# Which pairs of a SwiGLU projection use seven products, and where their fourth sum and their gated product stand

## The chip, the core and the metric

The kernel runs on one core of a Trainium2 chip. The metric is the time of one execution in microseconds (us), as the device measures it. A profile of one execution comes with its own time and its span, which is the time from the first instruction to the last. Times without a unit below are microseconds. TensorE (PE) multiplies matrices, and its weight loads are listed as PEld. VectorE is DVE, ScalarE is ACT, GpSimd is POOL, and SyncE (SP) issues most of the loads. Each of them works through its own queue of instructions.

## The reference

One layer of a streaming encoder for 256 positions of a new stream and 64 positions of a running one, 320 columns in all, with 2048 features. The part that the change touches is the feed-forward block:

```python
h = x + merged @ w_out[l]
hn = rmsnorm(h, norm_ffn[l])
gu = hn @ w_gate_up[l]
h = h + (jax.nn.silu(gu[..., :D_FF]) * gu[..., D_FF:]) @ w_down[l]
```

`D_FF` is 5632, so `w_gate_up` has 44 blocks of 128 gate columns and 44 of 128 up columns, and `w_down` has 44 blocks of 128 rows. All values are float32.

## The kernel before

Features lie on the 128 partitions and the 320 positions in the free dimension. float32 precision is made from 16-bit numbers: each weight block is scaled by a power of two and split into a high half (ScalarE, `Group.high`, line 373) and a low half (VectorE, `Group.low`, line 376), and the activations likewise. A product of a 128 x 128 block is then three matmuls of 320 columns, high by high, high by low, low by high (`product`, lines 108 to 110).

The feed-forward part works through 44 **pairs**, each a block of gate columns and the block of up columns that goes with it, over 16 blocks of input features. They are cut into three slices of 16, 16 and 12 pairs. Behind the first three pairs of the next slice (`AHEAD`) comes the down projection of a slice: 16 blocks, each with 16 (or 12) blocks of weights. Below, pair 1.4 is pair 4 of slice 1, counted from 0 within its slice; that is also how the table `FAST` counts.

An **ordinary** pair is a `Group` of two units: 2 x 16 x 3 = 96 matmuls of 320 columns. A pair in `FAST` is a `Fast`, a **seven-product** pair: two-by-two blocks of weights and activations are multiplied with seven products in place of eight, in the terms that hold the two low halves. It has 32 matmuls of 320 columns (`whole`, line 416) and seven times 16 of 160 columns (`cross`, line 422). Four of the seven products have sums of weight blocks as weights, made on VectorE by `sum_up` (line 412). Sums 1, 2 and 3 are made when the pair begins. Sum 4 is written over sum 2, so it cannot begin before the matmuls of product 2 have read that; product 22 at the end of the pair reads sum 4. When the pair is done, `join` (lines 454 to 459) adds the pieces up, ScalarE makes the silu, and `out` (line 1178, or 1180 for an ordinary pair) multiplies gate by up and takes the maximum of it (line 206).

The order is written by the program itself. A step (`tick`) is 8 blocks of input features in a product, four to a pair. `at(step, fn, rank)` puts a function down for a later step, and within a step the functions run in the order of their ranks; what they issue goes to the end of each engine's queue. So for a pair that begins at step S: the loads 10 or 11 steps ahead, a bound of each unit two steps later (ScalarE, line 210, into the unused `junk`), the maximum and its rounding (`topmost`, `packed`, lines 216 and 218) at S - 7 for a seven-product pair and S - 6 for an ordinary one, a small matmul that spreads it over the partitions into the one buffer `row` (line 222) at S - 5 or S - 4, then `peak`, `down`, `up` (lines 226 to 228), the high halves (rank 2) and the low ones (rank 2). `gated` runs one step behind the end of a pair (rank 2), and `out` one step behind that (rank 3). When a slice's last product is made, its maxima are spread in the same way and its activations are split, three in a step, on ScalarE and VectorE (lines 170 and 171).

Of the kernel before, what the change touches and what calls it, by code (L numbers as in the profile page):

```python
# [16 lines left out]
P = 128  # L17
# [6 lines left out]
HALF = 8  # L24
# [6 lines left out]
QSCALE = 128.0 ** -0.5  # L31
WARM = 10
PLAIN = 3
FAST = (7, 9, 10, 12, 13, 15), (2, 4, 5, 7, 8, 10, 11, 13, 14), (2, 4, 5, 7, 8, 10, 11)
AHEAD = 3
BACK = 4
WHOLE = 6
# [14 lines left out]
def stream_step(ctx: ExitStack, tc: tile.TileContext, xT, w_in, w_a, w_b, w_out, w_gu, w_down,  # L52
# [10 lines left out]
    def acc():  # L63
        return psum.tile([P, 512], F32, tag="acc", bufs=3, name="acc")

    def aux():
        return psum.tile([P, 512], F32, tag="aux", bufs=4, name="aux")
# [8 lines left out]
    def at(tick, fn, *a, rank=5):  # L76
        if tick <= state["tick"]:
            fn(*a)
        else:
            later.setdefault(tick, []).append((rank, fn, a))  # L80

    def tick():
        state["tick"] += 1
        for _, fn, a in sorted(later.pop(state["tick"], ()), key=lambda x: x[0]):
            fn(*a)

    def after(n, fn, *a, rank=5):
        if n == 0:
            fn(*a)
        else:  # L90
            at(state["tick"] + n, fn, *a, rank=rank)
# [53 lines left out]
    def slot(shape=(T,), dt=F32R, name="S"):  # L145
        return big.tile([P, *shape], dt, tag="S", bufs=SLOTS, name=name)
# [28 lines left out]
    def t320(tag, bufs=2, dt=F32):  # L175
        return tmp.tile([P, T], dt, tag=tag, bufs=bufs, name=tag)
# [212 lines left out]
    class Fast(Group):  # L389
# [35 lines left out]
        def blocks(self, x):  # L425
            assert state["tick"] == self.start
            gate, up, more = acc(), aux(), aux()
            part = lambda ps, n: ps[:, n * N : (n + 1) * N]
            turn_of["seen"] = turn_of.get("seen", 0) + 1
            self.seen = tmp.tile([P, 2, N], F32, tag="seen" if turn_of["seen"] % 2 else "sq", bufs=1, name="seen")  # L430
            self.chain, self.other, self.third = (part(more, n) for n in range(3))
            w0, w1, s, mid = self.w[0][2], self.w[1][2], self.sums, HALF // 2
            at(self.start + 1, lambda: nc.scalar.copy(out=self.seen[:, 0], in_=self.chain), rank=0.8)
            self.cross(self.chain, w0, 0, x, 11, start=True, stop=True)
            self.whole(gate, 0, x)
            tick()
            self.whole(up, 1, x)
            self.cross(part(up, 0), w1, HALF, x, 4, stop=True)
            tick()
            self.cross(self.chain, s[2], 0, x, 2, stop=True)  # L440
            self.sum_up(4, w0[:, :, HALF * P :], s[2], s[2])
            self.cross(part(gate, 0), w0, HALF, x, 21)
            self.cross(self.other, s[1], 0, x, 1, range(0, mid), start=True)
            tick()
            self.cross(self.other, s[1], 0, x, 1, range(mid, HALF), stop=True)
            self.cross(self.third, s[3], 0, x, 3, start=True, stop=True)
            self.cross(part(gate, 1), s[4], 0, x, 22, stop=True)
            tick()
            return gate[:, :T], up[:, :T]
# [453 lines left out]
    for i, (kind, n) in enumerate(line):  # L903
        by_vector = (0,) if 4 <= i < 33 and i % 5 in (1, 3) or i > 40 and i % 3 == 2 else ()
        if kind == "in":
            g = Group([[(w_in[n][:, j * HALF * P : (j + 1) * HALF * P], HALF) for j in range(2)]], start, lambda: [mixed.undo], 11, by_vector)
        else:
            g = Group([[(w_a[n], H), (w_b[n], H)]], start, lambda: [aT.undo, bT.undo], 11, by_vector, True)
# [129 lines left out]
    for g in range(H):  # L1038
        ps, undo = block16(3 * H + g, mixed.half)
        at(state["tick"] + 1, lambda g=g, ps=ps, undo=undo: nc.scalar.activation(  # L1040
            out=us[g], in_=ps, func=AF.Gelu_apprx_tanh, scale=undo), rank=2)
# [24 lines left out]
    for m in range(KD):  # L1066
        g = groups.pop(("ab", m))
# [23 lines left out]
    for made, (kind, s, i) in enumerate(order):  # L1091
        s0, n = SLICES[s]
        pieces = lambda w, k0, n: [(w[:, (k0 + k) * P : (k0 + min(k + HALF, n)) * P], min(HALF, n - k)) for k in range(0, n, HALF)]
        if kind == "up":
            if i < PLAIN:
                groups[kind, s, i] = Plain(w_gu[i], KD, now), Plain(w_gu[KF + i], KD, now + 2)
            else:
                both = [pieces(w_gu[i], 0, KD), pieces(w_gu[KF + i], 0, KD)]
                if i - s0 in FAST[s]:
                    groups[kind, s, i] = Fast((w_gu[i], w_gu[KF + i]), now, lambda: [ffn.undo])  # L1100
                else:
                    groups[kind, s, i] = Group(both, now, lambda: [ffn.undo], 12 if i < FAST[0][0] else 11, (), tight=i >= FAST[0][0])
            now += 4
        else:
            if i % 2 == 0:
                g = Group([pieces(w_down[i], s0, n), pieces(w_down[i + 1], s0, n)], now, lambda s=s: [acts[s].undo], 11, (), True, True)
# [21 lines left out]
    for m in range(KD):  # L1128
        x = t320("ev")
# [31 lines left out]
    def gated(s, pg, pu, g):  # L1161
        t, u = t320("ev"), t320("bb")
        if g is None:
            nc.vector.tensor_tensor(out=t, in0=pg, in1=got["rh"], op=ALU.mult)
            nc.scalar.activation(out=t, in_=t, func=AF.Silu)
            nc.vector.tensor_tensor(out=u, in0=pu, in1=got["rh"], op=ALU.mult)
        else:
            fast = isinstance(g, Fast)
            if fast:
                g.join(pg, pu, t, u)  # L1170
            nc.scalar.activation(out=t, in_=t if fast else pg, func=AF.Silu, scale=g.undo)
            if not fast:
                nc.scalar.activation(out=u, in_=pu, func=AF.Copy, scale=g.undo)

        def out():
            r = slot(dt=F32, name="act")
            if isinstance(g, Fast):
                nc.vector.scalar_tensor_tensor(out=r, in0=u, scalar=g.undo, in1=t, op0=ALU.mult, op1=ALU.mult)
            else:
                nc.vector.tensor_tensor(out=r, in0=u, in1=t, op=ALU.mult)  # L1180
            acts[s].add(r)

        after(1, out, rank=3)

    def downed(s, i, ps, g):
        nc.vector.scalar_tensor_tensor(out=hs[i], in0=ps, scalar=g.undo, in1=hs[i], op0=ALU.mult, op1=ALU.add)
# [18 lines left out]
    for kind, s, i in order:  # L1205
        if kind == "up":
            if i < PLAIN:
                gate_w, up_w = groups.pop((kind, s, i))
                pg, pu, g = gate_w.block(hg), up_w.block(hg), None
            else:  # L1210
                g = groups.pop((kind, s, i))
                pg, pu = g.blocks(ffn) if isinstance(g, Fast) else (g.block(0, ffn.half), g.block(1, ffn.half))
            at(state["tick"] + 1, gated, s, pg, pu, g, rank=2)
            continue
        end = s == 2 and i == KD - 1
        g, u = groups.pop((kind, s, i))
# [147 lines left out]
```

## Time and profile before

| | us |
|---|---|
| median of 3 runs | 1599.82 (1599.57 to 1601.29) |
| the profiled execution, its own time | 1598.27 |
| its span | 1596.5 |
| TensorE busy (matmul) | 1573.1, 99% of the span |
| VectorE busy | 1198.5, 75% |
| ScalarE busy | 1090.8, 68% |
| granted TensorE clock, mean | 0.997 |

The busy time of matmuls is modelled: each is shown longer than the time until the next one begins, since they overlap. What a piece of work takes on TensorE is therefore read from the starts of matmuls, and an idle time in brackets is counted from the modelled end of the matmul before. In a row of the timeline stand the start, the time shown, the engine, the line, the operation, the tile written and those read, the shapes and how many, and in brackets the idle time ahead of it with what ended that.

### The profile page before, as it was taken

The page shows a single profiled execution, that of the slowest core. Times are in us where ns is not written, and L with a number is a line of the kernel's source. Part 1 is how long each engine was busy: PE and PEld are TensorE (multiplying, and loading weights), DVE is VectorE, ACT ScalarE, POOL GpSimd, SP SyncE. Part 2 cuts the span into 40 slices and gives each one's busy share as a digit, 9 for nine tenths or more (in the row PEclk, how much of TensorE's full clock was granted, in tenths as well). Part 3 has the DMA queues.
Part 4 walks back from the last instruction along what each step waited for, and adds up shares of the span by engine and source line. Part 5 has one row for each costly group of instructions (what it writes and reads, how often), then busy time and mean ns, then how long its engine had stood idle before and what let it go on. Part 6 is the DMA issues. An engine that isn't in the chain of part 4 may idle for free.

```text
span 1596.5 us, 30559 instructions
## 1 busy us (share of the span) xinstructions
PE 1573.1 (99%) x12759; PEld 1232.9 (77%) x12759; DVE 1198.5 (75%) x2097; ACT 1090.8 (68%) x1229; POOL 68.1 (4%) x80
## 2 busy tenths in 40 slices
PE   9999999999999999999999999999999999999997
PEld 9987777777777768879778877778888777788775
DVE  6789887977777766966968878557888765688775
ACT  6589888867556654846776677666776776666663
POOL 0110111100000000121000000000000000000000
PEclk9999999999999999999999999999999999999998
DMA  8567665654444444554544454444545544444441
GB/s 304 200 202 221 198 173 147 190 167 159 159 159 158 160 141 162 184 176 170 185 169 167 170 183 141 163 164 143 174 169 178 166 159 158 159 159 148 146 130 66
DMA packets 94186, 268.49 MB, mean 168 GB/s; under 512 B 28288, under 2 KB 34688, under 8 KB 88416
## 3 DMA queue, kind: packets, MB, share of 16 engines
q1 hardware_dynamic: 91600, 261.36, 49.6%
q0 software_dynamic: 1312, 3.80, 0.6%
q8 instruction: 99, 1.62, 0.4%
q10 hardware_dynamic: 1136, 1.39, 0.2%
q14 instruction: 39, 0.32, 0.1%
HBM read 256.03 MB, written 5.51 MB: 164 GB/s over the span
## 4 chain that ended last, share of the span: by engine, by line
PE 80%; DVE 11%; ACT 6%; issue 3%; DMA 1%; DVEq 0%; POOL 0%; SPq 0%; ACTq 0%
PE acc L108 23%; PE acc L110 23%; PE acc L109 23%; DVE w L376 4%; DVE sum L412 3%; PE aux L422 3%; ACT w L373 2%; PE aux L539 2%; PE aux L416 1%; PE acc L416 1%; PE acc L422 1%; ACT junk L210 1%; PE acc L539 1%; DVE tops L206 1%; DVE half L171 1%
## 5 line engine op out<-in xcount | busy, mean ns | idle before, releaser
L110 PE MATMUL acc<-half,w 128*128 128x320 f16 x2688 | 803.7, 299 | 1.2 <-DVE w L376 1.1
L108 PE MATMUL acc<-half,w 128*128 128x320 f16 x2688 | 803.8, 299 | 0.4 <-DVE gate L1054 0.3
L109 PE MATMUL acc<-half,w 128*128 128x320 f16 x2688 | 803.7, 299 | 0.0
L373 ACT ACTIVATE w<-raw,up 128x2048 f16<-128x2048 f32 (+1 forms) x216 | 425.4, 1970 | 313.7 <-PE acc L110 210.0
L376 DVE SCALAR_TENSOR_TENSOR w<-raw,up,w 128x2048 f16<-128x2048 f32 (+1 forms) x216 | 499.0, 2310 | 99.3 <-ACT w L373 97.3
L210 ACT ACTIVATE junk<-raw 128x2048 uint8<-128x2048 f32 (+1 forms) x190 | 354.3, 1865 | 5.7 <-DMA raw<-w_in 1.7
L110 PEld LDWEIGHTS <-w 128*128 128x128 f16 x2688 | 263.0, 98 | 103.8 <-DVE w L376 1.8
L108 PEld LDWEIGHTS <-w 128*128 128x128 f16 x2688 | 263.0, 98 | 103.7 <-issue 2.0
L109 PEld LDWEIGHTS <-w 128*128 128x128 f16 x2688 | 263.0, 98 | 97.5 <-issue 0.9
L226 DVE TENSOR_REDUCE peak<-row 128x1 f32<-128x128 f32 x159 | 45.7, 288 | 123.9 <-PE row L222 123.9
L422 PEld LDWEIGHTS <-sum 128*128 128x128 f16 x1408 | 98.5, 98 | 9.1 <-DVE sum L412 9.1
L416 PEld LDWEIGHTS <-w 128*128 128x128 f16 x704 | 68.3, 98 | 25.1
L422 PE MATMUL aux<-mix,sum 128*128 128x160 f16 x1056 | 80.7, 233 | 0.0
L422 PEld LDWEIGHTS <-w 128*128 128x128 f16 x1056 | 75.7, 98 | 2.5
L130 ACT CAST w<-raw 128x1024 fp32r<-128x1024 f32 x36 | 37.7, 1047 | 42.6 <-PE acc L110 29.5
L206 DVE TENSOR_REDUCE tops<-raw 128x1 f32<-128x2048 f32 x26 | 59.2, 2277 | 0.0
L412 DVE TENSOR_TENSOR sum<-w,sum 128x2048 f16<-128x2048 f16 x44 | 53.8, 1223 | 5.9 <-PE aux L422 4.5
L412 DVE TENSOR_TENSOR sum<-w 128x2048 f16<-128x2048 f16 x44 | 53.6, 1219 | 1.0
L416 PE MATMUL aux<-half,w 128*128 128x320 f16 x352 | 51.4, 299 | 0.0
L416 PE MATMUL acc<-half,w 128*128 128x320 f16 x352 | 51.4, 299 | 0.0
L133 DVE TENSOR_TENSOR w<-raw,w 128x1024 fp32r<-128x1024 f32 x36 | 44.4, 1236 | 5.0 <-ACT w L130 4.7
L108 PE MATMUL acc<-S,w 128*128 128x320 f32 x144 | 44.8, 311 | 0.0
(256 smaller groups left out, 1641.6 us busy)
## 6 DMA issues: line engine op xcount, KB each, us to landing
raw<-w_in SPq DMA_DIRECT2D x141, 512.0 KB, 4.7
raw<-w_gu SPq DMA_DIRECT2D x88, 512.0 KB, 4.6
raw<-w_gu SPq DMA_DIRECT2D x44, 1024.0 KB, 4.8
raw<-w_down SPq DMA_DIRECT2D x80, 512.0 KB, 4.0
raw<-w_out SPq DMA_DIRECT2D x32, 512.0 KB, 4.7
raw<-w_a SPq DMA_DIRECT2D x16, 512.0 KB, 3.6
raw<-w_b SPq DMA_DIRECT2D x16, 512.0 KB, 4.5
raw<-w_down SPq DMA_DIRECT2D x16, 256.0 KB, 4.0
```

The costliest lines, as they stand in the source:

```text
L108: nc.tensor.matmul(ps[:, :T], a, x[0], start=first, stop=False, skip_group_check=True)
L109: nc.tensor.matmul(ps[:, :T], a, x[1], start=False, stop=False, skip_group_check=True)
L110: nc.tensor.matmul(ps[:, :T], b, x[0], start=False, stop=last, skip_group_check=True)
L206: nc.vector.tensor_reduce(out=self.tops[:, i : i + 1], in_=src, axis=mybir.AxisListType.X, op=ALU.max, apply_absolute_value=True)
L210: nc.scalar.activation(out=junk, in_=src, func=AF.Abs, accum_out=self.tops[:, i : i + 1])
L226: nc.vector.tensor_reduce(out=top, in_=self.row[:, :P], axis=mybir.AxisListType.X, op=ALU.max)
L373: nc.scalar.activation(out=w[:, 0], in_=self.raw[u][:, : self.width[u]], func=AF.Copy, scale=self.scale.up)
L376: nc.vector.scalar_tensor_tensor(out=self.w[u][1], in0=self.raw.pop(u)[:, : self.width[u]], scalar=self.scale.up, in1=self.w[u][0], op0=AL ...
L412: nc.vector.tensor_tensor(out=self.sums[i], in0=a, in1=b, op=ALU.add)
L416: nc.tensor.matmul(ps[:, :T], self.w[u][0][:, k * P : (k + 1) * P], x.half[k][0], start=k == 0, stop=False, skip_group_check=True)
L422: nc.tensor.matmul(out, w[:, h, (j + k) * P : (j + k + 1) * P], x.mixed[t, k][1 - h], start=start and k + h == 0, stop=stop and k + h == H ...
L539: nc.tensor.matmul(first[b][h][:, :T], w[:, (h * n + j) * P : (h * n + j + 1) * P], xs[c + j][i], start=not last and c + j + i == 0, stop= ...
```

## The change

```diff
-FAST = (7, 9, 10, 12, 13, 15), (2, 4, 5, 7, 8, 10, 11, 13, 14), (2, 4, 5, 7, 8, 10, 11)
+FAST = (7, 8, 10, 11, 13, 14), (4, 5, 7, 8, 10, 11, 13, 14), (3, 4, 6, 7, 9, 10)
...
             self.cross(self.chain, w0, 0, x, 11, start=True, stop=True)
             self.whole(gate, 0, x)
+            at(self.start + 2, lambda: self.sum_up(4, w0[:, :, HALF * P :], s[2], s[2]), rank=2.5)
             tick()
             self.whole(up, 1, x)
             self.cross(part(up, 0), w1, HALF, x, 4, stop=True)
+            self.cross(self.chain, s[2], 0, x, 2, stop=True)
             tick()
-            self.cross(self.chain, s[2], 0, x, 2, stop=True)
-            self.sum_up(4, w0[:, :, HALF * P :], s[2], s[2])
             self.cross(part(gate, 0), w0, HALF, x, 21)
...
             acts[s].add(r)
 
-        after(1, out, rank=3)
+        after(1 + isinstance(g, Fast), out, rank=3)
```

Twenty pairs in place of 22 have seven products. In slice 1 pair 2 is dropped and the rest stay. In slice 2 pair 2 is dropped, pair 11 becomes ordinary, and the others begin with pair 3, the first behind the 12 blocks of the down projection. In slice 0 the pairs are moved, and the last pair of the slice is no longer one of them. `sum_up(4)` is put down at step 2 of the pair with rank 2.5, behind that step's low half (rank 2) and ahead of its products and maxima (rank 3), where it stood behind all of them. The matmuls of product 2 are issued a step earlier in the program; between the other matmuls of the pair they stand where they stood. The product of a seven-product pair is made two steps behind `gated` and that of an ordinary pair one step, as before.

On VectorE, at the fourth sum of pair 1.4 (the first pair of two with seven products, behind an ordinary one), the order before is this. The first row is the low half of the first unit of pair 1.5, the `act` row the product of the ordinary pair 1.3, and the last row the low half of the second unit of pair 1.5:

```order
L376 SCALAR_TENSOR_TENSOR w<-raw,up,w 128x2048
L216 TENSOR_REDUCE topmost<-tops 128x1
L218 TENSOR_SCALAR packed<-topmost 128x1
L1180 TENSOR_TENSOR act<-bb,ev 128x320
L206 TENSOR_REDUCE tops<-act 128x1
L412 TENSOR_TENSOR sum<-w,sum 128x2048
L376 SCALAR_TENSOR_TENSOR w<-raw,up,w 128x2048
```

And with the change, at the same place:

```order
L376 SCALAR_TENSOR_TENSOR w<-raw,up,w 128x2048
L412 TENSOR_TENSOR sum<-w,sum 128x2048
L216 TENSOR_REDUCE topmost<-tops 128x1
L218 TENSOR_SCALAR packed<-topmost 128x1
L1180 TENSOR_TENSOR act<-bb,ev 128x320
L206 TENSOR_REDUCE tops<-act 128x1
L376 SCALAR_TENSOR_TENSOR w<-raw,up,w 128x2048
```

The fourth sum has moved ahead of four instructions, which now stand between it and the low half of the pair behind.

On VectorE, at the fourth sum of the second pair, 1.5, the order before (the first `L376` row is the low half of the first unit of the ordinary pair 1.6, the `act` row the product of pair 1.4, and `peak` to `up` make the scale of a later pair):

```order
L218 TENSOR_SCALAR packed<-topmost 128x1
L376 SCALAR_TENSOR_TENSOR w<-raw,up,w 128x2048
L1178 SCALAR_TENSOR_TENSOR act<-bb,undo,ev 128x320
L206 TENSOR_REDUCE tops<-act 128x1
L412 TENSOR_TENSOR sum<-w,sum 128x2048
L226 TENSOR_REDUCE peak<-row 128x1
```

And with the change:

```order
L218 TENSOR_SCALAR packed<-topmost 128x1
L376 SCALAR_TENSOR_TENSOR w<-raw,up,w 128x2048
L412 TENSOR_TENSOR sum<-w,sum 128x2048
L1178 SCALAR_TENSOR_TENSOR act<-bb,undo,ev 128x320
L206 TENSOR_REDUCE tops<-act 128x1
L226 TENSOR_REDUCE peak<-row 128x1
```

The product of the first pair and its maximum have moved from ahead of the sum to behind it.

On TensorE, between the ordinary pairs 1.0 and 1.1 of the changed program (the down projection of slice 0 begins two pairs later), the maxima of the activations of slice 0 and those of the weights of pair 1.2 are now spread by two matmuls in a row:

```order
L110 MATMUL acc<-half,w 128x320
L222 LDWEIGHTS packed
L222 MATMUL row<-turner,packed 128x128
L222 LDWEIGHTS packed
L222 MATMUL row<-turner,packed 128x128
L108 LDWEIGHTS w
```

Before, the matmul for pair 1.2 stood a step earlier, with products of pair 1.0 between the two. The same holds between pairs 2.0 and 2.1.

## The prediction

> **What bounds the kernel now.** I read the busy times first, then what TensorE waited for, then the timeline of its matmuls.
>
> ```profile
> PE 1573.1 (99%) x12759; PEld 1232.9 (77%) x12759; DVE 1198.5 (75%) x2097; ACT 1090.8 (68%) x1229; POOL 68.1 (4%) x80
> PE acc L422 <- DVE sum L412: 6.9, 11, 2.7
> PE row L222 <- DVE peak L226: 1.7, 4, 0.5
> ```
>
> TensorE has 99% of the span: a microsecond of matmul more or less is one of span, and so is one in which it waits. The second row (total, times, longest) says that in the feed-forward part it waits 11 times for a sum of weights, all for the fourth sum of a pair. The timeline of pairs 1.4 and 1.5 (start, length shown, engine, line) shows one:
>
> ```profile
> 1094.79 1.27 PE L422 MATMUL aux<-half,w 128*128 128x160 f16 x16
> 1095.90 2.34 PE L416 MATMUL acc<-half,w 128*128 128x320 f16 x16
> ...
> 1101.35 1.27 PE L422 MATMUL aux<-mix,sum 128*128 128x160 f16 x16
> 1102.46 1.27 PE L422 MATMUL acc<-half,w 128*128 128x160 f16 x16
> ...
> 1106.94 1.27 PE L422 MATMUL aux<-half,w 128*128 128x160 f16 x16
> 1118.30 1.28 PE L422 MATMUL acc<-half,sum 128*128 128x160 f16 x16 [0.15 <-DVE sum L412]
> 1119.42 0.30 PE L108 MATMUL acc<-half,w 128*128 128x320 f16 x1
> 1132.52 0.58 PE L422 MATMUL aux<-half,w 128*128 128x160 f16 x6
> ```
>
> Sixteen matmuls of 160 columns start within 1.11 (1101.35 to 1102.46), 0.069 each; one is drawn with 0.233, so an idle time in brackets is 0.164 short. A pair that waits for nothing takes 1106.94 - 1094.79 = 12.15. Pair 1.5, right behind it, takes 1119.42 - 1106.94 = 12.48: 12.15 and a wait of 0.15 + 0.16, rounded 0.33 below. The ordinary pair behind takes 1132.52 - 1119.42 = 13.10. All 11 waits are 6.9 + 11 x 0.164 = 8.7. Two are long, and both stand in front of a down projection (pairs 1.2 and 2.2):
>
> ```profile
> 961.93 1.27 PE L422 MATMUL aux<-half,w 128*128 128x160 f16 x16
> 975.76 1.28 PE L422 MATMUL acc<-half,sum 128*128 128x160 f16 x16 [2.68 <-DVE sum L412]
> 1285.82 0.38 PE L422 MATMUL acc<-half,sum 128*128 128x160 f16 x3 [2.68 <-DVE sum L412]
> ```
>
> They are 2.68 + 0.16 = 2.84 each, 5.68 together. The other nine have 8.7 - 5.7 = 3.0, 0.33 each: they are the second pairs of two in a row (and no first pair waits).
>
> **Part 1: two pairs fewer, and the long waits.** Pairs 1.2 and 2.2 become ordinary: 13.10 - 12.15 = 0.95 each, **+1.90**. Their waits go: **-5.68**. What made the fourth sum late there:
>
> ```profile
> 968.21 2.34 DVE L376 SCALAR_TENSOR_TENSOR w<-raw,up,w 128x2048 f16<-128x2048 f32 x1
> 971.92 0.15 DVE L216 TENSOR_REDUCE topmost<-tops 128x1 f32<-128x2 f32 x1 [1.37 <-ACT junk L210]
> ...
> 973.10 1.47 DVE L171 SCALAR_TENSOR_TENSOR half<-act,act_up,half 128x320 f16<-128x320 f32 x3
> 974.48 1.22 DVE L412 TENSOR_TENSOR sum<-w,sum 128x2048 f16<-128x2048 f16 x1
> 975.62 0.55 DVE L171 SCALAR_TENSOR_TENSOR half<-act,act_up,half 128x320 f16<-128x320 f32 x1
> ```
>
> An idle 1.37 and the splits of the activations stood ahead of it. What is due next is the down projection, at 961.93 + 13.10 = 975.0 by these times. The low half at 968.21 is that of its first unit and ends 4.5 ahead; the last split ends at 976.2, and the matmuls that use it are the last sixteenth of a down block of 48 matmuls, half an ordinary pair's 13.10, so they begin 15/16 of 6.5 = 6.1 after 975.0. Four sums of 1.22 leave VectorE there as well, so I take nothing for a new wait; if the cover is not there, the 5.68 or part of it returns.
>
> [...]
>
> **Part 2: the fourth sum and the product.** The chain on VectorE from the fourth sum of a first pair to that of the second, in pairs 1.4 and 1.5:
>
> ```profile
> 1098.33 2.35 DVE L376 SCALAR_TENSOR_TENSOR w<-raw,up,w 128x2048 f16<-128x2048 f32 x1 [1.28 <-ACT w L373]
> 1101.05 0.16 DVE L216 TENSOR_REDUCE topmost<-tops 128x1 f32<-128x2 f32 x1 [0.37 <-ACT junk L210]
> 1101.24 0.16 DVE L218 TENSOR_SCALAR packed<-topmost 128x1 bf16<-128x1 f32 x1
> 1101.31 0.48 DVE L1180 TENSOR_TENSOR act<-bb,ev 128x320 f32<-128x320 f32 x1
> 1101.83 0.49 DVE L206 TENSOR_REDUCE tops<-act 128x1 f32<-128x320 f32 x1
> 1102.66 1.22 DVE L412 TENSOR_TENSOR sum<-w,sum 128x2048 f16<-128x2048 f16 x1 [0.34 <-PE aux L422]
> 1103.80 2.35 DVE L376 SCALAR_TENSOR_TENSOR w<-raw,up,w 128x2048 f16<-128x2048 f32 x1
> ...
> 1113.78 2.35 DVE L376 SCALAR_TENSOR_TENSOR w<-raw,up,w 128x2048 f16<-128x2048 f32 x1
> 1116.05 0.54 DVE L1178 SCALAR_TENSOR_TENSOR act<-bb,undo,ev 128x320 f32<-128x320 f32 x1
> 1116.63 0.49 DVE L206 TENSOR_REDUCE tops<-act 128x1 f32<-128x320 f32 x1
> 1117.03 1.22 DVE L412 TENSOR_TENSOR sum<-w,sum 128x2048 f16<-128x2048 f16 x1
> ```
>
> The first sum cannot begin before TensorE has read the old one (1102.46, and 0.2 later it starts). Behind it VectorE has work without a break but for one wait for ScalarE, which itself waits for VectorE's scale. So the second sum comes a fixed time after TensorE's place in the first pair, and 0.33 too late.
>
> The change does two things to this chain. Out of its end goes the product of the first pair: 1117.03 - 1116.05 = 0.98. The product of the ordinary pair ahead, though, keeps its step and rank 3, and the first fourth sum, now rank 2.5, overtakes it: `topmost`, `packed`, `act` and `tops`, which stood in a stretch where VectorE waits anyway (0.37 and 0.34), now come behind the sum and ahead of the low half of the second pair. At their spacing that is 0.19 + 0.07 + 0.52 + 0.40 (the last as from 1116.63 to 1117.03) = 1.18 into the chain. Net +0.20: such a second pair waits 0.53. No cover is left, since the sum at the head of the queue waits for TensorE with all of that behind it.
>
> In two kinds of second pair it is otherwise. Where two ordinary pairs follow, the maximum stood in the end of the chain as well:
>
> ```profile
> 1226.71 2.34 DVE L376 SCALAR_TENSOR_TENSOR w<-raw,up,w 128x2048 f16<-128x2048 f32 x1
> 1228.97 0.15 DVE L216 TENSOR_REDUCE topmost<-tops 128x1 f32<-128x2 f32 x1
> ...
> 1230.20 1.22 DVE L412 TENSOR_TENSOR sum<-w,sum 128x2048 f16<-128x2048 f16 x1
> ```
>
> Out goes 1230.20 - 1228.97 = 1.23, in comes 1.18, from a wait of 0.36 (0.20 in brackets at this place): 0.31. That holds for 0.14, 1.14 and 2.10 (a down projection behind 2.11 has the same order). Pair 2.4's first pair stands behind a down projection, with no product of an ordinary pair: only 0.26 comes in, 0.98 goes out, and it waits for nothing. Six pairs (0.8, 0.11, 1.5, 1.8, 1.11, 2.7) at 0.53, three at 0.31, one at 0: 4.1, against 3.0 now: **+1.1**. Bounds: 0 a pair if the chain has more room than I see, 0.33 + 1.18 = 1.51 if taking the product out gives nothing. I take the middle, since it is a sum of rows of this very chain. That first pairs stay free of waits rests on the 1.28 that VectorE idles at 1098.33: the delayed product adds 0.98 there. Pair 2.3 itself, behind a down projection, is taken as any first pair.
>
> [...]
>
> **Part 3: two rows at once.** The maxima of the activations and those of the next unit's weights are spread by a small matmul each into the one `row` buffer. With an ordinary pair at 1.2 and 2.2 its spread falls a step later, onto that of the activations (in front of 1.1 and 2.1). The trace has this elsewhere:
>
> ```profile
> 1491.83 0.22 PE L222 MATMUL row<-turner,packed 128*128 128x128 bf16 x1
> 1492.09 0.29 DVE L226 TENSOR_REDUCE peak<-row 128x1 f32<-128x128 f32 x1 [0.49 <-PE row L222]
> ...
> 1492.43 0.22 PE L222 MATMUL row<-turner,packed 128*128 128x128 bf16 x1 [0.38 <-DVE peak L226]
> ```
>
> From one to the other 0.60, of which 0.055 is the matmul itself: 0.55 lost, twice: **+1.1**. Bounds: 0, and 0.67 (the longest of the four such waits, 0.5 idle and 0.17).
>
> **Sum.** 1.90 - 5.68 + 1.1 + 1.1 = -1.6. The profiled execution (1598.27, span 1596.5) would be 1596.7; the median of the runs shown is 1.55 above that execution, so **1598.2**. That is 0.1% less, and 0.2% (3.2 us) is about what a measurement can tell from no change.
>
> **The rivals.** (a) The fourth sums come in time everywhere, 0 in part 2 in place of +1.1 and -3.0 more than now: 1.90 - 5.68 - 3.0 + 1.1 = -5.7, **1594.1**. For it: 0.98 does leave the chain, three times what is missing. Against: the 1.18 that enters. (b) The other side: the long waits come back in front of the down projections, because splits and ScalarE's bounds (the 1.37) fill these steps with or without sums. All of it: -1.6 + 5.68 = +4.1, **1603.9**; it is slower than before by 0.2% once 4.8 of the 5.68 return. Against: the 4.5 of room. (c) Taking the product out brings nothing, because the last low half of the chain turns out to be released late by ScalarE: six at 1.51, three at 1.54, one at 0.6 is 14.3 in place of 4.1: **1608.4**. Against: that low half starts right behind its forerunner now. That the change would not do what it says is excluded by the order of the instructions.
>
> **Chances.** The forecast 0.81, (a) 0.11, (b) 0.05, (c) 0.03. The forecast's own range is 0.2 in ten waits, 0.3 in the rows and 0.05% between runs: 1595.0 to 1601.0, which leaves out the rivals, 0.19 in all. Faster by over 0.2% (below 1596.6): (a) and 0.05 of the forecast, 0.16. Slower (above 1603.0): most of (b), (c): 0.07. Within: 0.77.
>
> **What would show it.** Pairs 1.2 and 2.2 take 13.1 and have no wait for a sum behind them; two rows at once before pairs 1.1 and 2.1 with idle 0.4; fourth-sum waits of 0.36 in brackets (0.53) at six pairs, 0.15 at three, none at 2.4; in the first pair the sum stands right behind the low half and waits some 2 for TensorE. Wrong if those brackets are empty (a), if TensorE waits at the first down block (b), or if they exceed 1 (c).

## The result, and the profile after

| | before | after |
|---|---|---|
| median of 12 runs each | 1599.88 (1598.09 to 1601.93) | 1596.09 (1595.99 to 1596.57) |
| profiled execution | 1598.27 | 1595.99 |
| its span | 1596.5 | 1594.2 |

The ratio is 0.9975, with an interval of 0.9967 to 0.9983: 0.25% faster by the medians, 3.8 us, where the forecast was 1598.2 and a gain of 0.1%. The two profiled executions differ by only 2.3. So there are two questions: whether the waits came out as forecast, and where the other 1.5 us of the medians are.

The page and the waits of TensorE after the change (total, times, longest):

```profile
PE 1574.7 (99%) x12663; PEld 1230.1 (77%) x12663; DVE 1184.3 (74%) x2079; ACT 1089.3 (68%) x1227; POOL 68.1 (4%) x80
PE row L222 <- DVE peak L226: 2.4, 6, 0.5
PE acc L422 <- DVE sum L412: 2.1, 6, 0.4
```

The waits for the fourth sum have fallen from 6.9 to 2.1; none is long any more, but the six that are listed are longer than the old short ones (the bracket drew 0.15 before, now 0.35). The waits for `row` have gone from four to six. TensorE in front of pair 1.1, at the first matmul of pair 1.2 and at the first of the down projection behind it:

```profile
949.10 0.22 PE L222 MATMUL row<-turner,packed 128*128 128x128 bf16 x1
949.70 0.22 PE L222 MATMUL row<-turner,packed 128*128 128x128 bf16 x1 [0.38 <-DVE peak L226]
...
962.85 0.30 PE L108 MATMUL acc<-half,w 128*128 128x320 f16 x1
...
975.89 0.22 PE L222 MATMUL row<-turner,packed 128*128 128x128 bf16 x1
975.95 0.30 PE L108 MATMUL acc<-half,w 128*128 128x320 f16 x1
```

The two rows stand 0.60 apart. The ordinary pair 1.2 takes 975.95 - 962.85 = 13.10, and no wait stands behind it. The timeline of TensorE at pairs 1.4, 1.5 and the ordinary pair behind:

```profile
1093.81 1.27 PE L422 MATMUL aux<-half,w 128*128 128x160 f16 x16
...
1101.48 1.27 PE L422 MATMUL acc<-half,w 128*128 128x160 f16 x16
...
1105.96 1.27 PE L422 MATMUL aux<-half,w 128*128 128x160 f16 x16
...
1117.52 1.28 PE L422 MATMUL acc<-half,sum 128*128 128x160 f16 x16 [0.35 <-DVE sum L412]
1118.64 0.30 PE L108 MATMUL acc<-half,w 128*128 128x320 f16 x1
```

The first pair takes 1105.96 - 1093.81 = 12.15, the second 1118.64 - 1105.96 = 12.68, which is 12.15 and 0.53. VectorE in the same place:

```profile
1097.35 2.35 DVE L376 SCALAR_TENSOR_TENSOR w<-raw,up,w 128x2048 f16<-128x2048 f32 x1 [1.28 <-ACT w L373]
1101.68 1.23 DVE L412 TENSOR_TENSOR sum<-w,sum 128x2048 f16<-128x2048 f16 x1 [1.98 <-PE aux L422]
1102.82 0.15 DVE L216 TENSOR_REDUCE topmost<-tops 128x1 f32<-128x2 f32 x1
1103.01 0.16 DVE L218 TENSOR_SCALAR packed<-topmost 128x1 bf16<-128x1 f32 x1
1103.08 0.48 DVE L1180 TENSOR_TENSOR act<-bb,ev 128x320 f32<-128x320 f32 x1
1103.59 0.49 DVE L206 TENSOR_REDUCE tops<-act 128x1 f32<-128x320 f32 x1
1104.00 2.34 DVE L376 SCALAR_TENSOR_TENSOR w<-raw,up,w 128x2048 f16<-128x2048 f32 x1
...
1116.24 1.22 DVE L412 TENSOR_TENSOR sum<-w,sum 128x2048 f16<-128x2048 f16 x1
1117.38 0.55 DVE L1178 SCALAR_TENSOR_TENSOR act<-bb,undo,ev 128x320 f32<-128x320 f32 x1
```

The first sum stands at the head of VectorE's queue and waits 1.98 for TensorE, while the maximum and product of the ordinary pair, which could have run, stand behind it: what they read of ScalarE's was done by 1100.03 (`junk`, the later of the two, at 1099.83 for 0.20), 1.65 before the sum began. They put 1104.00 - 1102.82 = 1.18 into the chain to the second sum. From sum to sum it is 1116.24 - 1101.68 = 14.56, against 14.37 before.

For all runs below I use one measure: the **feed-forward stretch** in the profiled execution, from the first matmul of pair 0.0 to the first of the last down block. After the change these two are

```profile
727.34 0.42 PE L108 MATMUL acc<-S,w 128*128 128x320 f32 x1
...
1577.22 0.30 PE L108 MATMUL acc<-half,w 128*128 128x320 f16 x1
```

849.88 us apart, and before they were at 727.67 and 1579.27, 851.60 apart: 1.72 less, where 1.6 was forecast. The other 0.6 of the difference between the two spans lies ahead of the stretch (0.33) and behind it (0.24), in code that the change doesn't touch.

### The profile page after: what moved, and what is told of

Its sections match the earlier page's. It is cut to its first block, busy times and chain, and to the rows that moved or that the text cites. A ratio compares the mean times of both kernels' runs of the same rounds, so it can differ in the third digit from the quotient of the medians.

```text
span 1594.2 us, 30363 instructions
## 1 busy us (share of the span) xinstructions
PE 1574.7 (99%) x12663; PEld 1230.1 (77%) x12663; DVE 1184.3 (74%) x2079; ACT 1089.3 (68%) x1227; POOL 68.1 (4%) x80
## 4 chain that ended last, share of the span: by engine, by line
PE 79%; DVE 10%; ACT 7%; issue 2%; DMA 0%; DVEq 0%; ACTq 0%; SPq 0%
PE acc L108 23%; PE acc L109 23%; PE acc L110 23%; DVE w L376 4%; ACT w L373 3%; DVE sum L412 3%; PE aux L422 3%; PE aux L539 2%; PE aux L416 1%; PE acc L416 1%; ACT junk L210 1%; PE acc L422 1%; PE acc L539 1%; DVE tops L206 1%; PE row L222 0%
## 5 line engine op out<-in xcount | busy, mean ns | idle before, releaser
L110 PE MATMUL acc<-half,w 128*128 128x320 f16 x2752 | 822.9, 299 | 1.2 <-DVE w L376 1.1
L108 PE MATMUL acc<-half,w 128*128 128x320 f16 x2752 | 822.9, 299 | 0.4 <-DVE gate L1054 0.3
L109 PE MATMUL acc<-half,w 128*128 128x320 f16 x2752 | 822.8, 299 | 0.0
L376 DVE SCALAR_TENSOR_TENSOR w<-raw,up,w 128x2048 f16<-128x2048 f32 (+1 forms) x216 | 499.0, 2310 | 107.4 <-ACT w L373 107.4
L422 PEld LDWEIGHTS <-sum 128*128 128x128 f16 x1280 | 89.6, 98 | 4.3 <-DVE sum L412 4.3
L422 PE MATMUL aux<-mix,sum 128*128 128x160 f16 x960 | 73.3, 233 | 0.0
L412 DVE TENSOR_TENSOR sum<-w,sum 128x2048 f16<-128x2048 f16 x40 | 48.9, 1223 | 21.2 <-PE aux L422 19.8
L412 DVE TENSOR_TENSOR sum<-w 128x2048 f16<-128x2048 f16 x40 | 48.7, 1218 | 1.0
L416 PE MATMUL acc<-half,w 128*128 128x320 f16 x320 | 46.7, 299 | 0.0
L416 PE MATMUL aux<-half,w 128*128 128x320 f16 x320 | 46.7, 299 | 0.0
```

Source lines behind the costliest of these rows:

```text
L108: nc.tensor.matmul(ps[:, :T], a, x[0], start=first, stop=False, skip_group_check=True)
L109: nc.tensor.matmul(ps[:, :T], a, x[1], start=False, stop=False, skip_group_check=True)
L110: nc.tensor.matmul(ps[:, :T], b, x[0], start=False, stop=last, skip_group_check=True)
L376: nc.vector.scalar_tensor_tensor(out=self.w[u][1], in0=self.raw.pop(u)[:, : self.width[u]], scalar=self.scale.up, in1=self.w[u][0], op0=AL ...
L412: nc.vector.tensor_tensor(out=self.sums[i], in0=a, in1=b, op=ALU.add)
L416: nc.tensor.matmul(ps[:, :T], self.w[u][0][:, k * P : (k + 1) * P], x.half[k][0], start=k == 0, stop=False, skip_group_check=True)
```

## The experiments

In every run pairs, waits and stretch are read as above. All differences between kernels are in the feed-forward part unless said otherwise.

| kernel | pairs with seven products | stretch expected | stretch measured | time, median |
|---|---|---|---|---|
| before | 22 | | 851.60 | 1599.67 |
| the change | 20 | 850.0 | 849.88 | 1596.09 |
| table alone | 20 | 849.3 | 849.25 | 1595.52 |
| fourth sum alone, old table | 22 | 847.6 | 847.87 | 1594.71 |
| table and product | 20 | 845.9 | 845.79 | 1592.07 |
| table and fourth sum | 20 | 849.9 | 849.86 | 1596.37 |
| the change, maxima a step later | 20 | 848.2 | 848.22 | 1597.40 |
| table and product, maxima later | 20 | 844.1 | 844.16 | 1590.47 |
| table and product, maxima at the old steps, 1.2 and 2.2 back | 22 | 842.8 | 842.82 | 1590.12 |
| one pair more, last maxima later | 23 | 841.3 | 841.32 | 1588.16 |

(The time of before is its median beside the first five experiments. Beside the later ones it was 1600.22 and 1600.17.)

### The parts of the change, one by one

**The table alone.** The kernel before, with the new `FAST`:

```diff
-FAST = (7, 9, 10, 12, 13, 15), (2, 4, 5, 7, 8, 10, 11, 13, 14), (2, 4, 5, 7, 8, 10, 11)
+FAST = (7, 8, 10, 11, 13, 14), (4, 5, 7, 8, 10, 11, 13, 14), (3, 4, 6, 7, 9, 10)
```

> The new table alone: the fourth sum and the gated product stand where they stood before the change. Chain theory (the fourth sum of a second pair comes a fixed count of VectorE work after TensorE's place in the first pair, and what counts is which operations stand in between): nothing enters and nothing leaves the chain, so the ten second pairs wait what second pairs waited before, 0.33 each, three of them 0.36, 3.4 in all against the 4.0 measured with the change. Feed-forward stretch (from the first pair of the first slice to the last down block) 849.88 - 0.6 = 849.3, and 1595.5 in time. Load theory (the waits follow from the number of seven-product pairs in a row and VectorE's total work, wherever the sum and the product stand): the same 4.0, stretch 849.9, 1596.1. If the order edits were what mattered most, the two long waits of 2.84 would be back somewhere and the stretch would be above 852.

Measured: 849.25 and 1595.52 (ratio 0.9973, 0.9963 to 0.9984). Seven second pairs wait 0.32 to 0.33 and three 0.36 to 0.37. From the first sum to the second it is the old time again:

```profile
1101.41 1.23 DVE L412 TENSOR_TENSOR sum<-w,sum 128x2048 f16<-128x2048 f16 x1 [0.35 <-PE aux L422]
...
1115.79 1.22 DVE L412 TENSOR_TENSOR sum<-w,sum 128x2048 f16<-128x2048 f16 x1
```

14.38 against 14.56 with the change. So the table alone does all that the change does and a little more; the two edits of the order together cost 0.6.

**The fourth sum alone, with the old table.** The kernel before, with this and nothing else:

```diff
+            at(self.start + 2, lambda: self.sum_up(4, w0[:, :, HALF * P :], s[2], s[2]), rank=2.5)
             tick()
             self.whole(up, 1, x)
             self.cross(part(up, 0), w1, HALF, x, 4, stop=True)
+            self.cross(self.chain, s[2], 0, x, 2, stop=True)
             tick()
-            self.cross(self.chain, s[2], 0, x, 2, stop=True)
-            self.sum_up(4, w0[:, :, HALF * P :], s[2], s[2])
```

> The old table with 22 seven-product pairs, and only the fourth sum moved (to behind a low half); the product stays. Chain theory: at pairs 1.2 and 2.2 the sum no longer stands behind the wait for ScalarE and the splits, so both waits of 2.84 are gone; the nine second pairs pay the 1.18 that enters and gain the 0.98 that leaves, 0.52 each, 4.7 in all. 851.60 - 8.7 + 4.7 = 847.6 for the stretch, time about 1594. Load theory (VectorE and ScalarE are full in the steps before a down projection, whatever the order): half or more of the 5.68 comes back, at the sum or at the first down block, stretch 850.5 or more.

Measured: 847.87 and 1594.71 (0.9968, 0.9956 to 0.9981). Both waits of 2.84 are gone with the pairs 1.2 and 2.2 still of the seven-product kind. VectorE in pair 1.2:

```profile
968.84 2.35 DVE L376 SCALAR_TENSOR_TENSOR w<-raw,up,w 128x2048 f16<-128x2048 f32 x1
971.10 1.22 DVE L412 TENSOR_TENSOR sum<-w,sum 128x2048 f16<-128x2048 f16 x1
972.54 0.15 DVE L216 TENSOR_REDUCE topmost<-tops 128x1 f32<-128x2 f32 x1 [0.22 <-ACT junk L210]
...
973.72 1.93 DVE L171 SCALAR_TENSOR_TENSOR half<-act,act_up,half 128x320 f16<-128x320 f32 x4
```

The sum is made before the wait for ScalarE and the splits, and TensorE runs through into the down projection. The steps ahead of it were never too full; the sum only stood behind work that was not urgent. Six second pairs pay for it as forecast, 0.51 each. Three of the nine came out otherwise: 0.30 at 1.14 and 2.11, and 0.86 at 0.13, where a sum that precedes the fourth begins 0.35 later than in its like; why is not settled.

So each of the two remedies removes the long waits by itself, and having both is a loss: with the sum moved, making ordinary pairs of 1.2 and 2.2 gives up 0.95 and 0.55 at each of them for nothing. (The stretches differ by 2.0 and not by 3.0, since this run also waits 0.5 more in its second pairs, and 0.45 more between the two rows in the last slice, which stand 1.05 apart instead of 0.60.)

**The table and the product, the sum at its old place.**

```diff
+FAST = (7, 8, 10, 11, 13, 14), (4, 5, 7, 8, 10, 11, 13, 14), (3, 4, 6, 7, 9, 10)
...
-        after(1, out, rank=3)
+        after(1 + isinstance(g, Fast), out, rank=3)
```

> The new table and the product a step on; the fourth sum stays at its old place. Chain theory: 0.98 leaves the chain and the 1.18 does not enter, and only 0.33 to 0.36 was missing: no second pair waits. Stretch 849.88 - 4.0 = 845.9, time about 1592.1, 4.0 better than the change. Load theory: the waits stay near 0.4 each, stretch 849.9 or little less.

Measured: 845.79 and 1592.07 (0.9953, 0.9939 to 0.9966). No row for a wait for `sum` is left among the waits of TensorE; what leads them is

```profile
PE row L222 <- DVE peak L226: 2.4, 6, 0.5
PE aux L717 <- DVE S L704: 1.7, 1, 1.7
```

The same chain on VectorE:

```profile
1099.02 0.48 DVE L1180 TENSOR_TENSOR act<-bb,ev 128x320 f32<-128x320 f32 x1
1099.54 0.49 DVE L206 TENSOR_REDUCE tops<-act 128x1 f32<-128x320 f32 x1
1100.37 1.23 DVE L412 TENSOR_TENSOR sum<-w,sum 128x2048 f16<-128x2048 f16 x1 [0.34 <-PE aux L422]
1101.51 2.35 DVE L376 SCALAR_TENSOR_TENSOR w<-raw,up,w 128x2048 f16<-128x2048 f32 x1
...
1113.76 1.22 DVE L412 TENSOR_TENSOR sum<-w,sum 128x2048 f16<-128x2048 f16 x1
```

The ordinary pair's product is made while VectorE would wait anyway, and from sum to sum it is 13.39: the old 14.37 less the 0.98 of the first pair's product. It has 0.65 to spare, the 0.98 less the 0.33 that was missing. The move of the sum took away 4.1 of what the move of the product had to give.

**The table and the fourth sum, the product at its old step.** The changed kernel with `after(1, out, rank=3)`.

> The changed kernel with the product back at its old step: the table and the moved fourth sum alone. Chain theory: the moved sum of a second pair (rank 2.5) already stands ahead of the first pair's product (rank 3) in the same step, so putting that product a step on does nothing more: the same waits (0.51 six times, 0.30 three times), stretch 849.9, time 1596.1. Rival (it is the later product that takes 0.98 out of the chain, and without it the waits are that much longer): six at 1.5, three at 1.3, one at 0.7, 9.6 more, stretch 859.5, time 1605.7.

Measured: 849.86 and 1596.37 (0.9976, 0.9967 to 0.9984), with the waits of the changed kernel pair by pair. In the presence of the moved sum the later product does nothing. The prediction gave the gain of 0.98 to the edit of the product, when either edit alone brings it.

### Two rows at once

**The maxima of the activations a step later.** The changed kernel, with

```diff
-                at(now + 1, self.scale.pack, rank=3)
-                at(now + 2, self.scale.spread, rank=1)
-                at(now + 3, self.close, rank=0.5)
+                at(now + 2, self.scale.pack, rank=3)
+                at(now + 3, self.scale.spread, rank=1)
+                at(now + 4, self.close, rank=0.5)
                 for k in range(self.n):
-                    at(now + 3 + k // 3, self.split, k, rank=3)
+                    at(max(now + 4, now + 3 + k // 3), self.split, k, rank=3)
```

> The changed kernel with one thing more: the maximum of the activations is packed, spread and closed one step later, and their first three splits go with the next three. The spread of the activations then no longer falls on the step of a spread of a weight unit. Theory that the one row buffer costs 0.55 each time two spreads stand back to back: three such places go (in front of 1.1, 2.1 and in the second slice's down projection), 1.6 less: stretch 848.2, time 1594.5. Rival (the idle is only shifted, TensorE makes it up at a later wait, or the later splits hold up the down projection): stretch 849.9 or more.

Measured: the stretch is 848.22, but the time 1597.40 (0.9983, 0.9975 to 0.9992), 1.3 more than with the change. The stretch begins 3.39 later, at 730.73. The same class serves the attention part, where no step was free for this; two of the waits that are new there:

```profile
299.27 0.22 PE L222 MATMUL row<-turner,packed 128*128 128x128 bf16 x1
300.76 0.22 PE L222 MATMUL row<-turner,packed 128*128 128x128 bf16 x1 [1.27 <-DVE peak L226]
...
646.50 0.22 PE L222 MATMUL row<-turner,packed 128*128 128x128 bf16 x1 [1.23 <-DVE peak L226]
```

So 0.55 for two rows in a row is shown (three places, 1.66), and my expectation of the whole time overlooked who else uses the function.

**The same for the feed-forward part alone.** On the kernel with table and product; the new argument of `Acts` is by how many steps its maxima and first splits are late, 0 if it isn't given:

```diff
-    acts = [Acts(n) for _, n in SLICES]
+    acts = [Acts(n, 1) for k, (_, n) in enumerate(SLICES)]
```

> The new table and the product a step on, the sum at its old place (as in the run that reached 1592.07), and the activations' maxima of the feed-forward part alone packed, spread and closed a step later (their first three splits too). The earlier run that shifted these steps everywhere gained 1.66 in the feed-forward stretch and lost 3.4 ahead of it. Theory that this loss comes from the same steps in the attention part and not from the feed-forward part: 845.79 - 1.65 = 844.1 for the stretch, nothing lost ahead, time 1590.4. Rival (the gain of 1.66 had a price elsewhere that follows it): 1592 or more.

Measured: 844.16 and 1590.47 (0.9939, 0.9925 to 0.9952). The gain stays and the loss ahead is gone.

### Putting pairs back

**Pairs 1.2 and 2.2 with seven products.** On the kernel with table and product (its maxima at the old steps); `early` chooses, for these two pairs, the place that the change gives to the sum, and the old step of the product:

```diff
+FAST = (7, 8, 10, 11, 13, 14), (2, 4, 5, 7, 8, 10, 11, 13, 14), (2, 3, 4, 6, 7, 9, 10)
...
+                    groups[kind, s, i].early = i - s0 == 2
...
+            if self.early:
+                at(self.start + 2, lambda: self.sum_up(4, w0[:, :, HALF * P :], s[2], s[2]), rank=2.5)
+                self.cross(self.chain, s[2], 0, x, 2, stop=True)
+                tick()
+            else:
...
+        after(1 + (isinstance(g, Fast) and not g.early), out, rank=3)
```

> As the run that reached 1592.07, but pairs 1.2 and 2.2 have seven products again, and at these two alone the fourth sum stands where the change puts it, behind the low half, and the product at its old step (22 pairs in all). Chain theory: at these two places there is no second pair behind, nothing is pushed into a chain, and the splits stand behind the sum: no wait, two pairs of 12.15 in place of 13.10 and no two rows at once there: 845.79 - 1.9 - 1.1 = 842.8, time 1589.1. Rival (the steps in front of a down projection are too full for a seven-product pair): up to 2.84 at each, 848.5 and 1594.8.

Measured: 842.82; 1590.12 (0.994, 0.9927 to 0.9952). No pair waits. The time is 1 above what was expected; in the profiled execution (1590.02) half of that lies ahead of the stretch, the rest behind it and outside the span. One of the five runs took 1593.16, for which there is no trace.

**One pair more.**

```diff
+FAST = (7, 8, 10, 11, 13, 14), (2, 3, 4, 6, 7, 9, 10, 12, 13, 15), (2, 3, 4, 6, 7, 9, 10)
...
-                    groups[kind, s, i].early = i - s0 == 2
+                    groups[kind, s, i].early = i - s0 in (2, 15)
...
+    acts = [Acts(n, k == 2) for k, (_, n) in enumerate(SLICES)]
```

> As the run before, with one pair of seven products more (1.15, last in its slice, its sum and product as at 1.2; the pairs of two in the second slice start at 1.3, behind the down projection, in place of 1.4) and the maxima of the last slice's activations a step later (the one place left with two rows at once). Chain theory: 842.8 - 0.95 - 0.55 = 841.3, time 1587.6. Rival (23 pairs is more than VectorE carries): new waits of 0.3 or more in second pairs or at 1.15, 843 or more, time 1589.3 or more.

Measured: 841.32 and 1588.16 (1587.95 to 1588.38; ratio to before 0.9924, 0.9912 to 0.9937). It is the best version that was run: 12.1 below the kernel before in the same set of runs and 7.9 below the change.

### What else the medians held

**The kernel before, three executions more,** unchanged. What was open: its runs scatter over 4 to 5 us, those of the change over 0.6.

> The kernel before, unchanged, for one more profiled execution. Its timed runs scatter from 1598.1 to 1603.3 with medians of 1599.7 to 1600.2, while those of the change and of the variants stay within 0.6; the profiled execution of before was one of its fastest (1598.27). If the extra 1 to 3 us come from the two idles of 2.84 in TensorE (theory A: TensorE is granted less of its clock behind them, or the idle itself varies), the pairs 1.2 and 2.2 or the down blocks behind them are longer here by what this execution is above 1598.3, with a granted clock below 1.00 there. If it is anywhere in the program (theory B), the extra time lies in other blocks, or ahead of the feed-forward part.

> As the run before it: a further execution of the unchanged kernel. Theory A: extra time at pairs 1.2 and 2.2 and right behind. Theory B: elsewhere, at another place in each execution.

> As the two runs before it: a third further execution of the unchanged kernel. Theory A: extra time at pairs 1.2 and 2.2 and right behind, in the same blocks as in the others. Theory B: elsewhere.

Measured: 1602.28, 1599.60 and 1600.05, with stretches of 854.91, 852.98 and 853.23 (851.60 in the first). All waits for the sum are as in the first execution, 2.83 to 2.84 and 0.32 to 0.37. What is longer is pair 1.2 or 2.2 and the down block behind it: both places in the first of the three, 2.2 in the second, 1.2 in the third, and no other block by more than 0.06 (in the first the stretch also begins 0.70 later). TensorE behind pair 1.2 in the third:

```profile
975.79 2.31 PE L422 MATMUL acc<-half,sum 128*128 128x160 f16 x16 [2.67 <-DVE sum L412]
977.90 0.31 PE L222 MATMUL row<-turner,packed 128*128 128x128 bf16 x1
978.01 0.47 PE L108 MATMUL acc<-half,w 128*128 128x320 f16 x1
978.27 0.47 PE L109 MATMUL acc<-half,w 128*128 128x320 f16 x1
...
979.27 0.30 PE L110 MATMUL acc<-half,w 128*128 128x320 f16 x1
979.40 0.30 PE L108 MATMUL acc<-half,w 128*128 128x320 f16 x1
```

Behind the idle a matmul of 320 columns takes 0.27 from start to start, twice the 0.13 to which it returns at 979.27. In the first of the three the windows show why (window, its length, then the busy times of PE, PEld, DVE, ACT and POOL, the granted clock, the DMA share and GB/s):

```profile
976.00:977.00 1.00, 0.56 (x8) 0.56 (x9) 1.00 (x4) 0.81 (x2) 0.00 (x0) 1.00 0.00 0
977.00:978.00 1.00, 1.00 (x14) 0.88 (x12) 1.00 (x1) 0.00 (x0) 0.00 (x0) 0.81 0.00 0
978.00:979.00 1.00, 1.00 (x6) 0.54 (x5) 1.00 (x1) 0.00 (x0) 0.00 (x0) 0.50 0.00 0
979.00:980.00 1.00, 1.00 (x5) 0.54 (x4) 0.76 (x4) 0.08 (x1) 0.00 (x0) 0.50 0.00 0
980.00:981.00 1.00, 1.00 (x5) 0.60 (x4) 0.00 (x0) 1.00 (x1) 0.00 (x0) 0.50 0.74 127
981.00:982.00 1.00, 1.00 (x9) 0.69 (x7) 0.00 (x0) 1.00 (x2) 0.00 (x0) 0.98 0.88 320
982.00:983.00 1.00, 1.00 (x10) 0.72 (x8) 0.83 (x3) 0.10 (x1) 0.00 (x0) 1.00 1.01 414
```

In the records of the granted clock it is 0.50 from 977.62 to 981.03, for 3.41. Over the four executions (2 idles each) that happened behind 4 of the 8 idles, and cost 1.68, 1.66, 1.41 and 1.63, added up over the matmuls that ran slow. In the mean that is 0.80 per idle and 1.6 per execution.

The first profiled execution of before had none: its granted clock is 1.00 from 4.7 to 1588.4, by when its last matmul has begun (1586.76), and its two idles, 2.91 each from start to start, lie in that. In length they do not differ from the others (2.83 to 2.84 in all eight); what parts the idles that bring it from those that do not is not shown here.

**One idle put back.** In the kernel with 1.2 and 2.2 put back, 1.2 gets the old place of the sum again:

```diff
-                    groups[kind, s, i].early = i - s0 == 2
+                    groups[kind, s, i].early = s == 2 and i - s0 == 2
```

> The kernel with 22 seven-product pairs and no wait for a sum (stretch 842.82, timed runs 1589.7 to 1590.3 and one of 1593.2), with one of the two long idles put back: at pair 1.2 the fourth sum stands at its old place, behind three splits of the activations; 2.2 stays as it was. In the four executions of the kernel before, TensorE was granted half its clock for about 3.3 us in 4 of the 8 places behind such an idle, which costs 1.4 to 1.7 there. Theory A (the idle itself brings the half clock, at some phase of it): the timed runs fall into two groups, at 1590.1 + 2.8 = 1592.9 and 1.65 higher at 1594.6, about as many in each, and the profiled execution shows either no slow matmul or some 3.3 us of them right behind the idle. Theory B (the half clock has another cause that was bound to that kernel): all runs near 1592.9, within 0.6.

Measured: 1592.19, 1592.48, 1594.56, 1594.92 and 1594.93. They fall into two groups, as theory A has it and theory B has not, with the centres 0.6 below and 0.2 above what was expected. They are 2.5 apart, 0.8 more than one half clock costs in the traces; that is not explained. The profiled execution (1594.56) has the idle and the slow matmuls behind it:

```profile
975.31 1.51 PE L422 MATMUL acc<-half,sum 128*128 128x160 f16 x16 [2.67 <-DVE sum L412]
976.61 0.31 PE L222 MATMUL row<-turner,packed 128*128 128x128 bf16 x1
976.72 0.47 PE L108 MATMUL acc<-half,w 128*128 128x320 f16 x1
976.99 0.47 PE L109 MATMUL acc<-half,w 128*128 128x320 f16 x1
```

Its stretch is 847.33: 842.82, 2.83 for the idle, and the 1.68 that is left for the half clock. In its windows the granted clock is 0.54 from 976 to 979 and 0.89 from 979 to 982, 1.00 before and after; that is half the clock for 3.4. That the idle brings the half clock is thus shown by putting it in and by taking it out: none of the other kernels has an idle like it in this part, with the change the granted clock is 1.00 from 4.7 to 1588.4, and the stretches of all of them are within 0.3 of sums that have no half clock in them.

## Why the prediction was right, and where it was not

**Part 1, two pairs fewer and the long waits: right.** Pairs 1.2 and 2.2 take 13.10 each, and TensorE goes through them into the down projection without a wait (of 1.2 the rows are shown above); the +1.90 and the -5.68 are what the trace shows. The remark that the 4.5 of room covers the splits held too. What the prediction didn't ask is whether the move of the sum alone would have removed the waits, as the run with the old table shows.

**Part 2, fourth sum and product: right in its numbers, pair by pair.** Six waits of 0.51 to 0.52 (forecast 0.53), three of 0.30 (0.31), none at 2.4 (0), 4.0 together (4.1). The price of 1.18 that enters the chain is exact. One attribution fell: the 0.98 that leaves was put down to the later product, and with the sum moved that edit has no effect. Rival (a), no wait anywhere, is what the table and the product give without the move of the sum; its time for that, 1594.1, carried the offset spoken of below, and 1592.07 was measured. Rivals (b) and (c) are refuted: no wait at the first down block, no bracket above 0.4.

**Part 3, two rows at once: right.** 0.55 each at 1.1 and 2.1, and it goes when the spread is moved.

**The sum: right.** -1.6 forecast for the stretch, -1.72 measured.

**From the sum to the time: wrong.** The step that failed is "the median of the runs shown is 1.55 above that execution, so 1598.2". It took the distance between one execution and the median for a property of the measurement that the changed kernel keeps. It was a cost of the two long idles: the half clock behind them, 1.6 in the mean over the four executions, which the profiled execution was free of by luck, and which goes when the idles go: the median of the change is only 0.10 above its own profiled execution. Without that step the forecast is the profiled execution less 1.6, 1596.7; 1596.09 was measured, and nearly all of the 0.6 left is the 0.57 outside the stretch. That error of 1.6 also decided the chances: at 1598.2 the change is within 0.2%, at 1596.7 on the edge of it, and measured it is 0.25% faster, so that 0.77 for no change that can be told and 0.16 for faster stood the wrong way round. The time was in the range, 1595.0 to 1601.0, by luck: that was made wide for other reasons.

There was a sign of it in what the prediction had: three timed runs of 1599.57 to 1601.29 and a profiled execution at 1598.27, below all of them.

## What to carry to other kernels

An instruction that waits for another engine should be put behind the work that is due and could run meanwhile, and ahead of work that is not due, not just early: at pairs 1.2 and 2.2 moving the sum ahead of the splits took away 2.84 each, but at the other pairs the same move, ahead of four short instructions that were ready, cost 4 us, and the table and the product without that move gained twice the time of the whole change. Undo each part of a change by itself; two remedies for one wait can make each other useless or harmful. When timed runs scatter and the profiled execution lies at their lower end, look for what the others have that it has not, before the distance is carried over to a new kernel.

## What the runs showed of the hardware

An idle of TensorE of 2.83 us between matmuls (2.9 from the start of the last to the start of the next) was followed by a granted clock of 0.50 in 5 of 9 profiled cases. It lasted 3.41 us where it is shown above (977.62 to 981.03), and a matmul of 320 columns took 0.27 us in it from start to start where it took 0.13 otherwise; the price was 1.4 to 1.7 us on top of the idle. In the three cases behind pair 1.2 whose windows were read (the first and the third further execution of before, and the kernel with one idle put back) it began 1.2, 0.0 and 0.9 us after work had begun again. What parts the five from the four, and whether it is the same in other places, is not shown here. No other gap had it behind it in the first profiled execution of before and in that of the change, where the granted clock is 1.00 from 4.7 to 1588.4: from start to start these gaps are up to 0.60 in the feed-forward part and up to 1.9 ahead of it (near 179).
